# adaLN vectors as row sums over transposed weights, in a two-layer retention and attention trunk

## The chip, the cores and the metric

One core of a Trainium2 chip runs the whole kernel. The metric is the time of one execution on the device in microseconds; the median over runs is compared.

## The reference

A sequence of 512 tokens with 1024 features passes two layers. Layer 0 mixes tokens by multi-scale retention (4 heads), layer 1 by chunked attention with a relative bias (16 heads). Both start with an RMS norm that is modulated by a condition vector c, the same for all tokens, and both end with a gated residual:

```
cond = silu(c)                                   # [1024]
for i in range(2):
    mod = cond @ ada_w[i] + ada_b[i]             # [1024] x [1024, 3072]
    shift, scale, gate = split(mod, 3)
    h = rms_norm(x, norm_g[i]) * (1 + scale) + shift
    out = retention(h) if i == 0 else attention(h)   # h @ w_in, mixing, * silu gate, @ w_out
    x = x + gate * out
```

All data are float32. The six vectors (shift, scale and gate of both layers) are matrix-vector products with 24 MB of weights in all.

## The kernel before

TensorE does the large products in float32r. Every operand is split into two parts, a high one (a copy by ScalarE, `hi`) and a low one (a subtraction, mostly by VectorE, `lo`), and each 128x512 product is three matmuls. `load` fetches 512 rows by 512 columns of weights through SyncE's queue into one of two `raw` buffers (L258), and makes `whi` (L266, ScalarE) and `wlo` (L267); for output projections GpSimd first multiplies the weights by the gate (L263). In the last half of the last output projection GpSimd also does the low part (`low=nc.gpsimd`).

The products run as units of 12 matmuls. `go` runs a list of units; `at(u, fn)` hangs other work behind unit u. The tile framework then plans the order of every engine's queue with a timeline simulation, by the priority of program order and by when it takes data to be ready; `tc.issue_after` forces an order. A tile's `bufs` says how many buffers its tag has, and a tile whose buffer is still in use waits.

**The start.** h of layer 0 is made by quarters of the features. `norm_x` loads x, squares and scales it, and TensorE transposes it into `xT`. `prepare(s)` makes scale and shift of 256 features (`ada_256`), two rows of h of 128 features (L442) with their split, and the first weights for these rows. The eight 128x256 pieces of an adaLN weight are multiplied by cond, one value per partition, and added up: on VectorE (L412, L415) for all shifts and the first scale, on ScalarE and GpSimd (L418, L420) for the other scales. `column_sums` then sums over the partitions with matmuls against ones (L162). The products of quarter s (`first[0]`, the first values, and `first[1]`, the first queries) run while quarter s + 1 is prepared.

**The side vectors.** The gate of layer 0 and all vectors of layer 1 are made in 16 pieces, one behind every fourth unit of layer 0 (`side_piece`). Their weights go through `ada_load` (L126), 1 MB at a time, into the same two `raw` buffers as the projection weights; eight steps on VectorE (L148, L150) sum 512 columns. Layer 1's scale and shift are then transposed (L169) and reduced. A gate is split and spread to all partitions by two matmuls with ones (L201, L202); its bias is loaded by GpSimd (L141) into the first row of the sum.

```
for half in range(2):
    raw = ada_load(pool, layer, col, half)
    for k in range(4):
        ...
            nc.vector.scalar_tensor_tensor(acc, raw[:, k, :], c1, acc, ALU.mult, ALU.add)
```

Other lines that are named below: rotary products on VectorE (`rt`, L532, L537), head outputs of layer 0 (L618, L625), and in layer 1 the scores (`as`, L787), their addition of the bias with a running maximum (L790, one instruction that writes out and accumulates) and the transposed probabilities (`pth`, `ptl`).

Of the kernel before, what the change touches and what calls it, by code (L numbers as in the profile page):

```python
# [37 lines left out]
def f32(ap):  # L38
    return ap.bitcast(F32)
# [3 lines left out]
def hybrid_trunk_kernel(  # L43
# [3 lines left out]
    c_t: bass.AP,  # L47
    positions: bass.AP,
    norm_t: bass.AP,
    ada_w: bass.AP,  # L50
    ada_b: bass.AP,
# [24 lines left out]
    ct = cp.tile([P, NK], F32, name="ct")  # L76
    nc.sync.dma_start(ct, c_t)
# [21 lines left out]
    cond = cp.tile([P, NK], F32, name="cond")  # L99
    with tc.high_priority():  # L100
        nc.scalar.activation(cond, ct, AF.Silu)
# [8 lines left out]

    gs = cp.tile([P, 2, NK], F32, name="gs")
# [12 lines left out]
    def ada_load(pool, layer, col, half):  # L124
        raw = pool.tile([P, 4, 512], F32, tag="raw", name=f"ada_{layer}_{col}_{half}")
        nc.sync.dma_start(  # L126
            raw,
            ada_w[layer, half * 512 : (half + 1) * 512, col : col + 512].rearrange(
                "(k p) n -> p k n", p=P
            ),  # L130
        )
        return raw

    def ada_acc(pool, layer, col):
        """sum over k-tiles of cond * ada_w on every partition: [P, 512], in two steps;
        a gate's bias stands in the sum of the first partition."""
        acc = np_.tile([P, 512], F32, tag="acc", name=f"acc_{layer}_{col}", bufs=1)
        gate = col >= 2 * D
        if gate:
            nc.gpsimd.memset(acc, 0.0)  # L140
            nc.gpsimd.dma_start(acc[0:1, :], ada_b[layer : layer + 1, col : col + 512])  # L141
        for half in range(2):
            raw = ada_load(pool, layer, col, half)
            for k in range(4):
                kt = half * 4 + k
                c1 = cond[:, kt : kt + 1]
                if kt == 0 and not gate:
                    nc.vector.tensor_scalar(acc, raw[:, k, :], c1, None, ALU.mult)  # L148
                else:
                    nc.vector.scalar_tensor_tensor(acc, raw[:, k, :], c1, acc, ALU.mult, ALU.add)  # L150
            if half == 0:
                yield
        yield acc

    def column_sums(blocks, name, direct=False):
        """blocks: lists of [P, P]; the sums over their partitions, as [P, blocks]."""
        n, z = len(blocks), len(blocks[0])
        if direct:
            ps = pa.tile([P, n], F32, tag="pa", name=name)
            for j, parts in enumerate(blocks):  # L160
                for i, a in enumerate(parts):
                    mm = nc.tensor.matmul(  # L162
                        ps[:, j : j + 1], a, ones[:, 0:1], start=i == 0, stop=i == z - 1
                    )
            return ps, mm
        ps = pa.tile([P, n, z * P], F32, tag="pa", name=name)
        for j, parts in enumerate(blocks):
            for i, a in enumerate(parts):
                mm = nc.tensor.transpose(ps[:, j, i * P : (i + 1) * P], a, ident)  # L169
        sums = sp.tile([P, n], F32, tag=f"sums{n}", name=f"sums_{name}")  # L170
        nc.vector.tensor_reduce(sums, ps, mybir.AxisListType.X, ALU.add)
        return sums, mm

    def ada_finish(layer, col, accs, n):
        """n * 128 columns of scale or shift, summed over the partitions and laid over them."""
        c0 = col // P
        ps, mm = column_sums([[a[:, j * P : (j + 1) * P] for a in accs] for j in range(n)], f"mod_{layer}_{col}", layer == 0)
        if col < D:
            nc.vector.tensor_tensor(sh[:, layer, c0 : c0 + n], ps, bt[:, layer, c0 : c0 + n], ALU.add)
        else:  # L180
            tmp = sp.tile([P, n], F32, tag="mods", name="mods")
            nc.vector.tensor_tensor(tmp, ps, bt[:, layer, c0 : c0 + n], ALU.add)
            d0 = c0 - NK
            nc.vector.scalar_tensor_tensor(
                gs[:, layer, d0 : d0 + n], tmp, 1.0, ng[:, layer, d0 : d0 + n], ALU.add, ALU.mult
            )
        return mm

    def ada(pool, layer, col):
        """512 columns: scale and shift laid over the partitions, the gate on each of them."""  # L190
        for acc in ada_acc(pool, layer, col):
            if acc is None:
                yield
        if col < 2 * D:
            ada_finish(layer, col, [acc], 4)
        else:
            ps = pa.tile([P, 512], F32, tag="pa", name=f"gp_{layer}_{col}")
            hi = np_.tile([P, 512], F32R, tag="nat", name=f"gh_{layer}_{col}")
            lo = np_.tile([P, 512], F32R, tag="nat", name=f"gl_{layer}_{col}")
            split(hi, lo, acc)  # L200
            nc.tensor.matmul(ps, ones_r, hi, start=True, stop=False)  # L201
            nc.tensor.matmul(ps, ones_r, lo, start=False, stop=True)  # L202
            nc.scalar.activation(gates[layer][:, col - 2 * D : col - 2 * D + 512], ps, AF.Copy)
        yield

# [1 line left out]
    def norm_rows(t, tag, scalar=False):  # L207
        """x / rms(x), in two halves of the columns."""
# [39 lines left out]
    def load(parts, name, width=512, scale=None, w=None, k0=0, k1=4, low=None):  # L248
        """k-tiles k0..k1 of a piece of 4; parts: (columns of the tile, rows of the weights)."""
# [40 lines left out]
    class Chunk:  # L290
        """Columns of an input projection; cols: list of (columns of the tile, first column)."""
# [39 lines left out]
    # Products run as units of 12 matmuls; the other work is hung behind given units.  # L331
# [22 lines left out]
    def out_proj(name, w_out, row0, ys, gate, store=None, t_outer=False, done=None, rstd=None):  # L354
        ws = [None, None]

        def unit(half, t):
            csl = slice(half * 512, (half + 1) * 512)
            if ws[half] is None:
                ws[half] = load(  # L360
                    [(ALLC, w_out[row0 : row0 + 512, csl])], f"{name}_{half}", scale=gate[:, csl],
                    low=nc.gpsimd if store is not None and half else None,
                )
# [29 lines left out]
    with tc.tile_pool(name="st", bufs=1) as st:  # L393
        xT = st.tile([P, NK, S], F32, name="xT")

        def ada_256(col, name, vector, behind=None):
            raw = st.tile([P, NK, 256], F32, tag=f"ada_{name}", name=f"ada_0_{col}", bufs=3)
            for half in range(2):
                nc.sync.dma_start(
                    raw[:, half * 4 : half * 4 + 4, :],  # L400
                    ada_w[0, half * 512 : half * 512 + 512, col : col + 256].rearrange(
                        "(k p) n -> p k n", p=P
                    ),
                )
            accs = []
            for kt in range(NK):
                c1 = cond[:, kt : kt + 1]
                src = raw[:, kt, :]
                if vector and kt < 2:
                    acc = st.tile([P, 256], F32, tag=f"acc{kt}_{name}", name=f"acc{kt}_{col}")  # L410
                    accs.append(acc)
                    nc.vector.tensor_scalar(acc, src, c1, None, ALU.mult)  # L412
                elif vector:
                    acc = accs[kt % 2]
                    nc.vector.scalar_tensor_tensor(acc, src, c1, acc, ALU.mult, ALU.add)  # L415
                else:
                    with tc.issue_after(behind.ins) if behind else nullcontext():
                        nc.scalar.activation(src, src, AF.Copy, scale=c1)  # L418
                    if kt:
                        nc.gpsimd.tensor_tensor(raw[:, 0, :], raw[:, 0, :], src, ALU.add)  # L420
            return ada_finish(0, col, accs if vector else [raw[:, 0, :]], 2)
# [545 lines left out]
```

## Time and profile before

| what | value |
|---|---|
| median of 3 runs | 1000.54 us (996.72 to 1001.76) |
| span of the profiled execution | 996.1 us |
| mean granted TensorE clock | 0.986 |
| TensorE busy | 963.9 us (97%) |
| VectorE, ScalarE, GpSimd busy | 608.7, 384.3, 212.1 us |
| moved by DMA | 111.26 MB |

The span is from the first to the last instruction of one execution; of what lies around it the profile gives no time of its own, and the median of the runs is 4.4 us above it. Busy shares are averages over a start, two layers and a tail with different limits, so stretches and waits are read beside them.

### The profile page before, as it was taken

The page shows a single profiled execution, that of the slowest core. Times are in us where ns is not written, and L with a number is a line of the kernel's source. Part 1 is how long each engine was busy: PE and PEld are TensorE (multiplying, and loading weights), DVE is VectorE, ACT ScalarE, POOL GpSimd, SP SyncE. Part 2 cuts the span into 40 slices and gives each one's busy share as a digit, 9 for nine tenths or more (in the row PEclk, how much of TensorE's full clock was granted, in tenths as well). Part 3 has the DMA queues.
Part 4 walks back from the last instruction along what each step waited for, and adds up shares of the span by engine and source line. Part 5 has one row for each costly group of instructions (what it writes and reads, how often), then busy time and mean ns, then how long its engine had stood idle before and what let it go on. Part 6 is the DMA issues. An engine that isn't in the chain of part 4 may idle for free.

```text
span 996.1 us, 11965 instructions
## 1 busy us (share of the span) xinstructions
PE 963.9 (97%) x4572; PEld 803.9 (81%) x4572; DVE 608.7 (61%) x1012; ACT 384.3 (39%) x813; POOL 212.1 (21%) x205
## 2 busy tenths in 40 slices
PE   4999979999999999999999999999999999999988
PEld 3778868888778888888788888888888888888876
DVE  6977789558862563766445566545556346556683
ACT  6433413232223333426344445234543244444431
POOL 4810231004200103612100270002520012004520
PEclk8799989999999999999999999999999999999999
DMA  9645534653262222222232222223223232213202
GB/s 336 215 129 188 180 126 129 193 196 124 89 209 98 85 85 84 85 85 85 93 104 71 74 96 96 96 85 93 73 78 97 84 96 90 90 56 99 91 1 85
DMA packets 80537, 111.26 MB, mean 112 GB/s; under 512 B 12016, under 2 KB 44832, under 8 KB 80480
## 3 DMA queue, kind: packets, MB, share of 16 engines
q1 hardware_dynamic: 68368, 102.77, 31.3%
q0 software_dynamic: 10960, 5.63, 2.1%
q10 hardware_dynamic: 1152, 2.10, 0.6%
q8 instruction: 36, 0.59, 0.2%
q14 instruction: 21, 0.17, 0.1%
HBM read 108.32 MB, written 2.10 MB: 111 GB/s over the span
## 4 chain that ended last, share of the span: by engine, by line
PE 81%; DVE 8%; DMA 5%; issue 3%; POOL 1%; ACT 1%; SPq 0%; POOLq 0%; DVEq 0%; ACTq 0%
PE pm_aqk L277 6%; PE pm_aqk L275 6%; PE pm_aqk L276 6%; PE ao L827 3%; PE as L787 3%; PE pm_av L276 3%; PE pm_av L277 3%; PE pm_av L275 3%; PE po_a L277 3%; PE po_a L276 3%; PE po_a L275 3%; PE pm_ag L283 3%; DVE acc L150 3%; PE pm_ag L284 3%; PE pm_ag L285 3%; DMA ada<-in_ada_w_dram 3%
## 5 line engine op out<-in xcount | busy, mean ns | idle before, releaser
L275 PE MATMUL pm_aqk<-whi_aqk,hTh 128*128 128x512 f32 x256 | 101.8, 398 | 0.0
L277 PE MATMUL pm_aqk<-whi_aqk,hTl 128*128 128x512 f32 x256 | 100.5, 393 | 0.0
L276 PE MATMUL pm_aqk<-wlo_aqk,hTh 128*128 128x512 f32 x256 | 100.3, 392 | 0.0
L150 DVE SCALAR_TENSOR_TENSOR acc<-ada,cond,acc 128x512 f32<-128x512 f32 x60 | 52.9, 882 | 22.5 <-DMA ada<-in_ada_w_dram 11.5
L275 PE MATMUL pm_rv<-whi_rv,hTh 128*128 128x512 f32 x128 | 52.3, 413 | 5.4 <-ACT hTh L350 5.4
L277 PEld LDWEIGHTS pm_aqk<-whi_aqk,hTl 128*128 128x128 f32 x256 | 48.1, 188 | 10.1
L775 POOL DMA_DIRECT2D br<-in_att_bias_dram x16 | 13.4, 837 | 200.3 <-DVE nm L794 172.1
L275 PEld LDWEIGHTS pm_aqk<-whi_aqk,hTh 128*128 128x128 f32 x256 | 48.1, 188 | 9.5
L276 PEld LDWEIGHTS pm_aqk<-wlo_aqk,hTh 128*128 128x128 f32 x256 | 48.2, 188 | 9.3
L267 DVE TENSOR_TENSOR wlo_aqk<-raw_aqk,whi_aqk 128x2048 fp32r<-128x2048 f32 x16 | 36.6, 2289 | 30.3 <-ACT whi_aqk L266 30.3
L796 ACT ACTIVATE p<-p,nm 128x128 f32<-128x128 f32 (+1 forms) x64 | 35.9, 563 | 49.3 <-DVE nm L794 48.3
L263 POOL TENSOR_TENSOR raw_r<-raw_r,gate 128x2048 f32<-128x2048 f32 x8 | 39.5, 4937 | 72.1 <-DMA raw_r<-in_ret_w_out_dram 70.5
L275 PE MATMUL po_r<-whi_r,yh 128*128 128x512 f32 x128 | 51.8, 407 | 1.5 <-DVE rt L532 1.5
L790 DVE CUSTOM_DVE_ANT_0 p<-as,br 128x128 f32<-128x128 f32 (+1 forms) x64 | 30.4, 486 | 36.8 <-PE as L787 33.9
L276 PE MATMUL pm_rv<-wlo_rv,hTh 128*128 128x512 f32 x128 | 52.4, 409 | 0.0
L276 PE MATMUL po_r<-wlo_r,yh 128*128 128x512 f32 x128 | 51.7, 404 | 0.0
L277 PE MATMUL po_r<-whi_r,yl 128*128 128x512 f32 x128 | 51.6, 403 | 0.0
L285 PE MATMUL pm_rqk<-hTh,wlo_rqk 128*128 128x512 f32 x128 | 49.7, 391 | 1.8 <-DVE wlo_rqk L267 1.8
L283 PE MATMUL pm_ag<-hTh,whi_ag 128*128 128x512 f32 x128 | 50.7, 398 | 0.0
L283 PE MATMUL pm_rqk<-hTh,whi_rqk 128*128 128x512 f32 x128 | 50.7, 397 | 0.0
L284 PE MATMUL pm_ag<-hTl,whi_ag 128*128 128x512 f32 x128 | 50.4, 394 | 0.0
L277 PE MATMUL pm_rv<-whi_rv,hTl 128*128 128x512 f32 x128 | 50.3, 401 | 0.0
(219 smaller groups left out, 2622.3 us busy)
## 6 DMA issues: line engine op xcount, KB each, us to landing
ada<-in_ada_w_dram SPq DMA_DIRECT2D x16, 1024.0 KB, 5.1
raw_aqk<-in_att_w_in_dram SPq DMA_DIRECT2D x32, 512.0 KB, 4.6
ada<-in_ada_w_dram SPq DMA_DIRECT2D x16, 512.0 KB, 8.4
raw_rg<-in_ret_w_in_dram SPq DMA_DIRECT2D x8, 1024.0 KB, 5.1
raw_r<-in_ret_w_out_dram SPq DMA_DIRECT2D x8, 1024.0 KB, 5.0
raw_ag<-in_att_w_in_dram SPq DMA_DIRECT2D x8, 1024.0 KB, 5.4
raw_av<-in_att_w_in_dram SPq DMA_DIRECT2D x8, 1024.0 KB, 5.3
raw_a<-in_att_w_out_dram SPq DMA_DIRECT2D x8, 1024.0 KB, 5.1
```

Of the source, the lines that this page charges most:

```text
L150: nc.vector.scalar_tensor_tensor(acc, raw[:, k, :], c1, acc, ALU.mult, ALU.add)
L263: nc.gpsimd.tensor_tensor(raw, raw, scale.unsqueeze(1).broadcast_to([P, k1 - k0, width]), ALU.mult)
L267: (low or nc.vector).tensor_tensor(lo, raw, f32(hi), ALU.subtract)
L275: nc.tensor.matmul(ps, a_h, wh[:, k, :], start=first and k == 0, stop=False)
L276: nc.tensor.matmul(ps, a_h, wl[:, k, :], start=False, stop=False)
L277: nc.tensor.matmul(ps, a_l, wh[:, k, :], start=False, stop=last and k == 3)
L283: nc.tensor.matmul(ps, wh[:, k, csl], h, start=first and k == 0, stop=False)
L284: nc.tensor.matmul(ps, wh[:, k, csl], l, start=False, stop=False)
L285: nc.tensor.matmul(ps, wl[:, k, csl], h, start=False, stop=last and k == 3)
L787: nc.tensor.matmul(ps[:, :w0], a[:, qsl], b[:, :w0], start=z == 0, stop=z == 2)
L790: nc.vector.tensor_tensor_reduce(p[:, :w], ps[:, :w], br[:, S - w :], 1.0, -3.0e38, ALU.add, ALU.max, mx)
L796: nc.scalar.activation(p[:, :w], p[:, :w], AF.Exp, bias=nm, accum_out=sm)
```

## The change

The weights of the adaLN vectors come transposed from the host (`ada_t`, one row per feature), and cond lies on all partitions as a row of 1024. A vector's values of 128 features are then one VectorE instruction that multiplies a [128, 1024] tile of weight rows by cond and sums along the row into a column of `mod` (`ada_dot`). No sum over partitions is left for scale and shift. A gate has to be spread to all partitions: 128 values become a diagonal matrix (`diag`, two buffers), and TensorE multiplies it with ones in fp32, four times per 512 features. In the start VectorE does all of the sums and all steps that make h, weights come in 1 MB loads into six buffers, and the forced orders go. The side vectors have two buffers of their own (`ada`, 4 KB per partition); each block's load is hung four units ahead of its sum. The low part of the last weights goes to VectorE. Two one-column tiles share one tile of 64 columns, and the scratch for GpSimd's transfer descriptors shrinks from its default to 4096 bytes per partition.

```diff
-    ct = cp.tile([P, NK], F32, name="ct")
-    nc.sync.dma_start(ct, c_t)
+    cond = cp.tile([P, D], F32, name="cond")
+    nc.sync.dma_start(cond, c_row.broadcast_to([P, D]))
...
-        nc.scalar.activation(cond, ct, AF.Silu)
+        nc.scalar.activation(cond, cond, AF.Silu)
...
+    def ada_dot(raw, layer, block):
+        nc.vector.tensor_tensor_reduce(
+            raw, raw, cond, 1.0, 0.0, ALU.mult, ALU.add, mod[:, layer, block : block + 1]
+        )
+    def ada_finish(layer, b0, n):
+        m, b = mod[:, layer, b0 : b0 + n], bt[:, layer, b0 : b0 + n]
+        if b0 < NK:
+            nc.vector.tensor_tensor(sh[:, layer, b0 : b0 + n], m, b, ALU.add)
+            return
+        nc.vector.tensor_tensor(m, m, b, ALU.add)
+        if b0 < 2 * NK:
+            g0 = b0 - NK
+            nc.vector.scalar_tensor_tensor(
+                gs[:, layer, g0 : g0 + n], m, 1.0, ng[:, layer, g0 : g0 + n], ALU.add, ALU.mult
+            )
+            return
+        ps = pa.tile([P, n, P], F32, tag="pa", name=f"gp_{layer}_{b0}")
+        for j in range(n):
+            diag = np_.tile([P, P], F32, tag="diag", name=f"diag_{layer}_{b0 + j}", bufs=2)
+            nc.vector.tensor_scalar(diag, ident, m[:, j : j + 1], None, ALU.mult)
+            nc.tensor.matmul(ps[:, j, :], ones, diag, start=True, stop=True)
+        g0 = (b0 - 2 * NK) * P
+        nc.scalar.activation(
+            gates[layer][:, g0 : g0 + n * P], ps.rearrange("p a b -> p (a b)"), AF.Copy
+        )
...
-        (low or nc.vector).tensor_tensor(lo, raw, f32(hi), ALU.subtract)
+        nc.vector.tensor_tensor(lo, raw, f32(hi), ALU.subtract)
...
+        def ada_256(b0):
+            raw = st.tile([P, 2, D], F32, tag="ada", name=f"ada_0_{b0}", bufs=6)
+            nc.sync.dma_start(
+                raw, ada_t[0, b0 * P : (b0 + 2) * P, :].rearrange("(b p) k -> p b k", p=P)
+            )
+            for j in range(2):
+                ada_dot(raw[:, j, :], 0, b0 + j)
+            ada_finish(0, b0, 2)
...
-                (nc.vector if kt in (1, 3) else nc.gpsimd).tensor_scalar(
+                nc.vector.tensor_scalar(
...
-        _, h0 = prepare(0)
+        prepare(0)
         for s in range(3):
             ws = [ch.w for ch in first]
-            for u in range(4):
-                first[0].unit(s // 2, u, ks(s))
-            mm, _ = prepare(s + 1, None if s else h0)
-            with tc.issue_after(mm.ins):
-                new, first[1].w = first[1].w, ws[1]
-                for u in range(2):
-                    first[1].unit(s // 2, u, ks(s))
-                first[1].w = new
+            prepare(s + 1)
+            for ch, w in zip(first, ws):
+                new, ch.w = ch.w, w
+                for u in range(ch.n):
+                    ch.unit(s // 2, u, ks(s))
+                ch.w = new
...
+            tiny = rp.tile([P, 64], F32, name="tiny")
+            ifr, hpi = tiny[:, 0:1], tiny[:, 1:2]
...
-        for z in range(16):
-            at(now[0] + 2 + 4 * z, side_piece)
+        def side_load(layer, block):
+            raw = np_.tile([P, D], F32, tag="ada", name=f"ada_{layer}_{block}", bufs=2)
+            nc.sync.dma_start(raw, ada_t[layer, block * P : (block + 1) * P, :])
+            held[layer, block] = raw
+        def side_dot(layer, block):
+            ada_dot(held.pop((layer, block)), layer, block)
+            if block % 4 == 3:
+                ada_finish(layer, block - 3, 4)
+        held = {}
+        blocks = [(0, 16 + b) for b in range(8)]
+        blocks += [(1, b) for b in (*range(8, 16), *range(8), *range(16, 24))]
+        for z, (layer, block) in enumerate(blocks):
+            u = 2 + 2 * z if z < 8 else 20 + (z - 8) * 7 // 2
+            at(max(u - 4, 0), side_load, layer, block)
+            at(u, side_dot, layer, block)
...
-    nc = _bacc.Bacc("TRN2", target_bir_lowering=False, num_devices=1)
+    nc = _bacc.Bacc(
+        "TRN2", target_bir_lowering=False, num_devices=1, dynamic_dma_scratch_size=4096
+    )
```

## Rows read from the trace of the kernel before

**Rows 1.** Busy time by stretch: engine, busy us, instructions; granted clock, DMA share.
```profile
0.00:25.00 25.00, 10.46 (x55) 9.31 (x56) 15.15 (x40) 17.31 (x39) 10.93 (x26) 0.90 0.96 336
25.00:50.00 25.00, 22.69 (x86) 18.41 (x85) 23.54 (x36) 11.95 (x26) 20.16 (x22) 0.76 0.59 213
...
125.00:150.00 25.00, 19.85 (x78) 15.81 (x77) 21.39 (x26) 4.25 (x5) 8.19 (x3) 0.86 0.34 126
```

**Rows 2.** What TensorE waited for: us in total, times, longest us.
```profile
PE hp L431 <- DVE xn L225: 9.9, 1, 9.9
PE pm_rv L275 <- ACT hTh L350: 5.4, 2, 3.1
PE mod L169 <- DVE acc L150: 3.9, 1, 3.9
PE as L787 <- DVE ptl L351: 2.5, 1, 2.5
PE pm_rqk L285 <- DVE wlo_rqk L267: 1.8, 1, 1.8
...
PE po_r L275 <- DVE rt L532: 1.5, 2, 1.3
```

**Rows 3.** 9 to 57 us: VectorE alone, then all engines' instructions on adaLN tiles.
```profile
9.00:57.00 48.00, 43.34 (x81) 0.82 0.73 255
...
9.00:57.00 48.00, 1.85 (x12) 2.29 (x12) 23.36 (x40) 9.87 (x24) 18.61 (x21) 0.82 0.73 255
```

**Rows 4.** VectorE in order of time: start, us, line, operation, idle time before.
```profile
14.52 3.24 DVE L415 SCALAR_TENSOR_TENSOR acc<-ada,cond,acc 128x256 f32<-128x256 f32 x8
...
18.34 1.22 DVE L267 TENSOR_TENSOR wlo_rv<-raw_rv,whi_rv 128x1024 fp32r<-128x1024 f32 x1
...
21.86 0.69 DVE L351 TENSOR_TENSOR hTl<-h,hTh 128x512 fp32r<-128x512 f32 x1 [1.18 <-ACT hTh L350]
...
24.08 5.41 DVE L415 SCALAR_TENSOR_TENSOR acc<-ada,cond,acc 128x256 f32<-128x256 f32 x6
```

**Rows 5.** All engines and DMA from 11 to 37 us.
```profile
11.00:37.00 26.00, 19.02 (x95) 15.93 (x94) 24.64 (x48) 18.91 (x41) 15.04 (x18) 0.87 1.08 388
```

**Rows 6.** The chain of waits, 40 to 56 us: start, us, what.
```profile
40.65 1.44 PE mod L162 x6
...
45.28 0.43 PE pm_rv L275
...
48.09 0.23 PE pm_rv L275
```

**Rows 7.** VectorE in layer 1: an instruction that accumulates, 512 columns.
```profile
967.60 0.68 DVE L790 CUSTOM_DVE_ANT_0 p<-as,br 128x512 f32<-128x512 f32 x1
968.21 0.08 DVE L790 DVE_READ_ACCUMULATOR2_ANT mx<- 128x1 f32 x1
```

**Rows 8.** TensorE in order of time: idle time before and who ended it.
```profile
21.88 0.79 PE L275 MATMUL pm_rv<-whi_rv,hTh 128*128 128x512 f32 x1 [3.10 <-ACT hTh L350]
...
60.47 0.39 PE L275 MATMUL pm_rv<-whi_rv,hTh 128*128 128x512 f32 x1
...
142.22 0.52 PE L169 MATMUL mod<-ident,acc 128*128 128x128 f32 x3 [3.88 <-DVE acc L150]
```

**Rows 9.** Idle time of engines before adaLN steps, and a wait of SyncE's queue.
```profile
  DMA ada<-in_ada_w_dram: 17.8, 8
...
SPq L258 <- DVE wlo_aqk L267: 189.2, 15, 22.3
```

**Rows 10.** GpSimd and VectorE at the same time, at 124 and at 961 us.
```profile
123.59 5.11 POOL L263 TENSOR_TENSOR raw_r<-raw_r,gate 128x2048 f32<-128x2048 f32 x1 [0.56 <-DVE yl L625]
...
124.16 5.08 DVE L150 SCALAR_TENSOR_TENSOR acc<-ada,cond,acc 128x512 f32<-128x512 f32 x1
...
960.45 4.58 POOL L267 TENSOR_TENSOR wlo_a<-raw_a,whi_a 128x2048 fp32r<-128x2048 f32 x1 [13.40 <-ACT whi_a L266]
...
961.09 4.09 DVE L799 TENSOR_SCALAR p<-p,ri 128x256 f32<-128x256 f32 x1
```

More of the change, by code (lines that the diff above doesn't have):

```diff
@@ L1 @@
 import math
-from contextlib import ExitStack, nullcontext
+from contextlib import ExitStack
 import numpy as np
@@ L46, in hybrid_trunk_kernel @@
     x: bass.AP,
-    c_t: bass.AP,
+    c_row: bass.AP,
     positions: bass.AP,
     norm_t: bass.AP,
-    ada_w: bass.AP,
-    ada_b: bass.AP,
+    ada_t: bass.AP,
     ada_bt: bass.AP,
@@ L97, in hybrid_trunk_kernel @@
     nc.gpsimd.memset(mhalf, -0.5)
-    cond = cp.tile([P, NK], F32, name="cond")
     with tc.high_priority():
-        nc.scalar.activation(cond, ct, AF.Silu)
+        nc.scalar.activation(cond, cond, AF.Silu)
     kq = cp.tile([P, 1], F32, name="kq")
@@ L109, in new_h @@
         hT["l"] = hp.tile([P, NK, S], F32R, tag="hTl", name=f"hTl_{layer}")
+    mod = cp.tile([P, 2, 24], F32, name="mod")
     gs = cp.tile([P, 2, NK], F32, name="gs")
@@ L121, in rstd_of @@
         return rs
[L124 to L130, printed above, removed]
-        )
[L132 to L169, printed above, removed]
+    def ada_dot(raw, layer, block):
+        nc.vector.tensor_tensor_reduce(
+            raw, raw, cond, 1.0, 0.0, ALU.mult, ALU.add, mod[:, layer, block : block + 1]
+        )
@@ L170, in column_sums @@
+    def column_sums(blocks, name):
+        n = len(blocks)
+        ps = pa.tile([P, n, P], F32, tag="pa", name=name)
+        for j, a in enumerate(blocks):
+            nc.tensor.transpose(ps[:, j, :], a, ident)
         sums = sp.tile([P, n], F32, tag=f"sums{n}", name=f"sums_{name}")
         nc.vector.tensor_reduce(sums, ps, mybir.AxisListType.X, ALU.add)
[L172 to L204, printed above, removed]
+        return sums
@@ L245, in norm_tile, with load @@
             nc.vector.tensor_tensor(hT["l"][:, ksl, tsl], h, f32(hT["h"][:, ksl, tsl]), ALU.subtract)
-    def load(parts, name, width=512, scale=None, w=None, k0=0, k1=4, low=None):
+    def load(parts, name, width=512, scale=None, w=None, k0=0, k1=4):
         if w is None:
@@ L361, in unit @@
                     [(ALLC, w_out[row0 : row0 + 512, csl])], f"{name}_{half}", scale=gate[:, csl],
-                    low=nc.gpsimd if store is not None and half else None,
                 )
@@ L394, in hybrid_trunk_kernel @@
         xT = st.tile([P, NK, S], F32, name="xT")
[L396 to L421, printed above, removed]
+        def ada_256(b0):
[6 more added lines that the diff above has]
+            ada_finish(0, b0, 2)
         def norm_x():
@@ L434, in norm_x, with prepare @@
                     )
-        def prepare(s, behind=None):
-            ada_256(D + s * 256, "scale", s == 0, behind)
-            mm = ada_256(s * 256, "shift", True)
+        def prepare(s):
+            ada_256(NK + 2 * s)
+            ada_256(2 * s)
             for kt in (2 * s, 2 * s + 1):
                 h = np_.tile([P, S], F32, tag="nat", name=f"h_0_{kt}")
-                (nc.vector if kt in (1, 3) else nc.gpsimd).tensor_scalar(
+                nc.vector.tensor_scalar(
                     h, xT[:, kt, :], gs[:, 0, kt : kt + 1], sh[:, 0, kt : kt + 1], ALU.mult, ALU.add
                 )
-                last = split(hT["h"][:, kt, :], hT["l"][:, kt, :], h)
+                split(hT["h"][:, kt, :], hT["l"][:, kt, :], h)
             for ch in first:
                 ch.load(s // 2, ks(s))
-            return mm, last
         def ks(s):
@@ L489, in rope_tables @@
             nc.gpsimd.dma_start(posi, positions.broadcast_to([P, S]))
-            ifr = rp.tile([P, 1], F32, name="ifr")
+            tiny = rp.tile([P, 64], F32, name="tiny")
+            ifr, hpi = tiny[:, 0:1], tiny[:, 1:2]
             nc.gpsimd.dma_start(ifr, inv_freq)
-            hpi = rp.tile([P, 1], F32, name="hpi")
             nc.gpsimd.memset(hpi, math.pi / 2)
@@ L630, in norm_y @@
         def norm_y(n):
-            ps, _ = column_sums([[rstd[n][:, t * P : (t + 1) * P]] for t in range(NT)], f"ss_{n}")
+            ps = column_sums([rstd[n][:, t * P : (t + 1) * P] for t in range(NT)], f"ss_{n}")
             ms = sp.tile([P, NT], F32, tag="ms4", name=f"ms_{n}")
@@ L650, in outp @@
             return out_proj(f"r{n}", ret_w_out, n * 512, lambda: yy[n], gates[0], rstd=lambda: rstd[n], **kw)
-        side = [ada(wp, *a) for a in (
-            (0, 2 * D), (0, 2 * D + 512), (1, D), (1, D + 512), (1, 0), (1, 512),
-            (1, 2 * D), (1, 2 * D + 512),
-        )]
-        def side_piece():
-            if side:
-                g = side[0]
-                k = side_n[0] = side_n[0] + 1
-                next(g)
-                if k % 2 == 0:
-                    side.pop(0)
-        side_n = [0]
-        for z in range(16):
-            at(now[0] + 2 + 4 * z, side_piece)
+        def side_load(layer, block):
[13 more added lines that the diff above has]
+            at(u, side_dot, layer, block)
         rope_tables()
@@ L892 @@
 _INS = [
-    "x", "c_t", "positions", "norm_t", "ada_w", "ada_b", "ada_bt", "ret_w_in", "ret_gn_t", "ret_w_out",
+    "x", "c_row", "positions", "norm_t", "ada_t", "ada_bt", "ret_w_in", "ret_gn_t", "ret_w_out",
     "att_w_in", "att_qg_t", "att_kg_t", "att_bias", "att_w_out", "inv_freq", "decay",
@@ L936 @@
         "x": np.asarray(x)[0],
-        "c_t": np.asarray(c).reshape(NK, P).T,
+        "c_row": np.asarray(c).reshape(1, D),
         "positions": np.asarray(positions),
         "norm_t": np.asarray(norm_g).reshape(2, NK, P).transpose(2, 0, 1),
-        "ada_w": ada_w,
-        "ada_b": ab,
+        "ada_t": np.asarray(ada_w).transpose(0, 2, 1),
         "ada_bt": ab.reshape(2, 24, P).transpose(2, 0, 1),
```

## Prediction

> **What bounds the kernel now.** I read the busy time by stretch first. TensorE is busy nearly all the time except in two places: the first 50 us, where 0:25 has 10.46 us of work and 25:50 a mean granted clock of 0.76, and 125:150, with 19.85 us of 25 and a clock of 0.86 [rows 1]. Any gain must come from there, or from a stall too short to show in a stretch.
>
> The waits of TensorE, longest in total first, name them [rows 2]: 9.9 us for normalised x before the first transposes, 5.4 us for the rounded half of h, 3.9 us for an adaLN accumulation (L150), 2.5 us for a split in the last layer, 1.8 us for a weight split, 1.5 us for the rotary products. All of these producers sit on VectorE or right behind it.
>
> In the start, 9 to 57, VectorE is busy 43.34 of 48 us; 23.36 us of that works on adaLN tiles, beside 9.87 us of ScalarE and 18.61 us of GpSimd on the same tiles [rows 3]. The reader is to see that the two engines disturb each other: eight L415 steps take 3.24 us, 0.405 each, while GpSimd is quiet, and six take 5.41 us, 0.90 each, while it adds [rows 4]. DMA moves 388 GB/s from 11 to 37 us [rows 5]: the 13 MB that the start needs (x 2, adaLN 8, weights 3) take 33.5 us at that rate, and beginning at 2 to 5 us they bring the last block at 36 to 39. Until then data limits the start, VectorE and TensorE after it.
>
> A TensorE pause is paid twice. In the chain of waits a 512-column matmul takes 0.43 us at 45 us and 0.23 at 48 [rows 6]: the granted clock is at its lower level, 1.2 GHz, after the stalls ahead of it, and at 2.4 later.
>
> **The change, part by part.** *Row sums.* 512 columns of one vector cost eight VectorE steps before, plus column sums on TensorE. Now four instructions of 128x1024 do it, with the sum in `mod`. No such instruction is in the trace. From below: a plain two-input step of 128x1024 takes 1.22 us [rows 4]. From the same family: L790, which also writes out and accumulates, takes 0.68 at 512 columns and 0.08 for reading the accumulator [rows 7], so one more 512 columns (1.22 - 0.69 = 0.53) give 0.68 + 0.53 + 0.08 = 1.29. From above: twice the plain step, 2.44. I take 1.3, by the row of the same operation.
>
> A rule speaks for the upper end. The Trainium skill (Vector Engine (DVE) Microarchitecture Reference, section Points that are easy to get wrong) says that a scalar-tensor-tensor step with two SBUF sources that aren't bf16 runs at half rate, for want of a port for the accumulator. The quiet L415 steps have two such sources and 0.405 us for 256 columns, not half the rate of the plain step; but they don't use the accumulator, and L790 reads one source from PSUM, so no run here shows the case itself. By the rule the 16 blocks of the start would take 39 us instead of 21.
>
> *Start.* Layer 0's scale and shift are 16 blocks: 16 x 1.3 = 20.8 us of VectorE in place of 23.36, and the 9.87 us on ScalarE, the 18.61 on GpSimd and 26 column-sum matmuls (two instructions each, 0.24 at the lower clock [rows 6]) go. All eight h steps move to VectorE, six of them from GpSimd: at 0.45 us (one source, so less than the 0.69 of a two-input step of that width [rows 4]) that is +2.7 us. GpSimd being quiet, nothing else on VectorE is stretched. From about 11 us VectorE then has 20.8 (sums) + 8 x 0.45 (h) + 8 x 0.6 (low halves, the 0.69 overlaps the next by 0.09 [rows 4]) + 4 x 1.15 and 4 x 0.6 (weight splits) + 4 (small steps and x) = 40.2 us, and ends at 51 rather than 57.
>
> For TensorE I follow its order. First product: now 21.88 [rows 8], after an h step on GpSimd; with VectorE's shorter one and sums instead of column sums, about 20. Each of the four feature quarters has 36 matmuls, 8.2 us at 0.227. Quarter 0 starts at 20, about 12 of them at 0.43 (now the same), ends at 31. Quarter 1 has its h at about 28: 31 to 39. Quarter 2 has h at 38 and its weights at 39, since its buffers come free when quarter 1's value products end: 39 to 47.5. Quarter 3 needs h from the last two loads, which land at about 39 by the DMA rate, then four sums: 47 to 48, so it ends at 56.5. In the trace it starts at 60.47 and lasts as long [rows 8], ending at 68.7. Gain 12; as VectorE has no slack left there I take 10.5. Bounds: 2 (only the first product earlier) and 13.
>
> *The condition vector on all partitions.* A 512 KB load ahead of x instead of 4 KB, and a 128x1024 SiLU. At 388 GB/s [rows 5] it delays x and all behind it by 1.3 us; the SiLU takes 1 us of ScalarE ahead of the squares of x. Against that GpSimd no longer issues bias loads between the steps of the norm. Together 0 to 2 us; it is inside the 10.5. A source row read 128 times might come slower; the first scale block lands at 11, so 6 us are covered.
>
> *Own buffers.* The side vectors shared the two `raw` buffers and SyncE's queue with the weights, one MB at a time, issued when a buffer came free. VectorE stood still for them eight times, 17.8 us [rows 9]; once this reached TensorE, up to 142.22: 3.88 us [rows 8], 1.3 more for the rotary products behind it on VectorE [rows 2], then about 12 matmuls at the lower clock, 12 x 0.2 = 2.4 (the mean clock of 0.86 [rows 1] says 25 x 0.14 x 2 = 7 us at that level, pauses included). With loads of 512 KB issued four units ahead (4 x 12 x 0.227 = 10.9 us) and 1.3 us of work per block, none is late. Gain 7.5 (bounds 0 and 8). What is late next is the 4.6 to 5 us in which a GpSimd gate product holds a VectorE step: L263 123.59 to 128.7, L150 124.16 to 129.2 [rows 10]. This stays.
>
> *Gates by diagonals.* 16 VectorE steps of 128x128 (about 0.25 us) and 16 fp32 matmuls replace eight 128x512 matmuls (1.8 us) and four pairs of split steps. An fp32 product is two instructions; each costs at least the 0.12 of a column sum at full clock (half of 0.24) and at most a 512-column matmul, 0.23: 3.8 to 7.3 us. Net I add 2.5 us to TensorE (bounds 1 and 6: two `diag` buffers tie VectorE to TensorE's place, and a late VectorE holds TensorE). In layer 1, 16 transposes go; I leave them uncounted.
>
> *The last split on VectorE.* At 960.45 GpSimd runs it for 4.58 us and holds a 256-column VectorE step for 4.09 [rows 10]; TensorE waits 2.5 us [rows 2] and, as after the other pauses, restarts at the lower clock, for which I put 1 us. On VectorE it takes twice the 1.22 of half its width [rows 4], less overlap 2.3 us, and holds no one longer. Gain 2.5 (bounds 0 and 3.5).
>
> *The rest.* Shared tile for two tiny columns, smaller descriptor scratch, no forced issue order: nothing by any row; the work stays and few transfers come from GpSimd.
>
> **Sum.** -10.5 - 7.5 - 2.5 + 2.5 = -18. I add 1.5 for the 1.8 us wait for a weight split [rows 2], which moves to a place where VectorE has more to do. The instruction order is planned anew, so +-4. Span 996.1 - 16.5 = 979.6. The three runs shown are 996.7, 1000.5 and 1001.8; their median is 4.4 above the span. Keeping that distance: **984**.
>
> **Rivals.**
> 1. *VectorE stays the bound in the start*: sums at 2.44 us, or rotary tables and value splits that can't follow. At 2.44, 16 blocks add 18 us: VectorE ends near 69, quarter 3 ends at 75, 6.5 late instead of 12 early. With the 7.5, 2.5 and -2.5 of the rest the time is about 1000; with a mere half of the start's gain lost, 989. The half rate is what the skill's rule above would bring. For it: VectorE 43.34 of 48 busy [rows 3]. Against it: L790's row [rows 7].
> 2. *Every stall goes*: 13 + 8 + 3.5 - 1 = 23.5, and no new wait: 977. Also 973 if the short waits elsewhere shrink.
> 3. *Slower: sums at the head of VectorE's queue wait for late loads.* 32 block loads lie in SyncE's queue among weight loads that wait up to 22.3 us for their buffers [rows 9], twice the lead of 10.9 us; a sum in front of VectorE then holds splits and rotations. One such stall costs TensorE 3.9 + 1.3 + 2.4 = 7.6 us, as at 138. Against a gain of 18 it decides from the third on; with four it is 1000.5 - 16.5 + 30 = 1014. Against it: sums wait for one 512 KB load, not for 1 MB behind two weight tiles.
> 4. *No change*: the planner hides the start's gain in waits at about 70 us, and the gates take the rest: 1000.
>
> **How the numbers follow.** Main case 0.56: 978 to 990, predicted 984. Rival 2: 0.16, rival 1 with half the gain lost 0.12, with the sums at half rate 0.05, rival 4 0.05, rival 3 0.06. Within 0.5% (995.5 to 1005.5) is about what a measurement tells from no change. Faster 0.84, same 0.10, slower 0.06. The range holds the main case, rival 2 and the milder rival 1: 971 to 995; outside it lie 0.16.
>
> **What would show it.** Right: one 128x1024 sum near 1.3 us; no GpSimd adds before 57; first product near 20, the fourth quarter ended near 57; no TensorE wait above 2 us from 110 to 150 and a clock of 1.00 there; no GpSimd split near the end. Wrong: sums above 2 us; VectorE idle for `ada` loads; TensorE waiting for `diag`, `vl` or rotary products; the low clock in more stretches than before.

## The result: slower by 1%, where a gain of 1.6% was forecast

The changed kernel takes 1008.08 us (median of 4 runs, 1007.40 to 1010.44) against 998.85 us for the kernel before, run beside it (996.72 to 1001.76). The ratio is 1.0101, with a 95% interval of 1.0073 to 1.0130. The prediction was 984 us, range 971 to 995, with a chance of 0.06 for slower. It was wrong in sign. The profiled execution took 1008.13 us; its span rose from 996.1 to 1006.4 us, though TensorE's busy time fell from 963.9 to 961.0 us and VectorE's from 608.7 to 595.7: TensorE stands idle 13.2 us longer, and its mean granted clock falls from 0.986 to 0.980.

Busy time by stretch, changed kernel (columns as in [rows 1]):

```profile
0.00:25.00 25.00, 8.49 (x36) 6.93 (x37) 12.53 (x29) 16.04 (x33) 8.84 (x20) 0.86 0.93 350
25.00:50.00 25.00, 21.41 (x82) 17.06 (x81) 24.96 (x51) 6.40 (x10) 0.64 (x1) 0.86 0.81 311
50.00:75.00 25.00, 18.52 (x72) 14.42 (x71) 20.66 (x41) 5.44 (x8) 1.69 (x5) 0.82 0.64 194
75.00:100.00 25.00, 24.49 (x105) 19.78 (x105) 23.96 (x38) 8.16 (x9) 0.00 (x0) 0.98 0.84 303
100.00:125.00 25.00, 23.83 (x120) 20.12 (x118) 22.91 (x34) 7.26 (x10) 5.10 (x1) 1.00 0.63 216
125.00:150.00 25.00, 18.44 (x82) 15.58 (x83) 19.23 (x29) 6.95 (x10) 6.45 (x5) 0.86 0.61 184
150.00:175.00 25.00, 20.90 (x85) 16.75 (x85) 22.90 (x30) 6.73 (x7) 6.44 (x2) 0.86 0.28 95
```

The loss lies before 175 us. 50:75, 125:150 and 150:175 now have 18 to 21 us of TensorE work and a granted clock of 0.82 to 0.86, and VectorE is busy for 20.7 to 25.0 us of every 25 from 25 to 125. What TensorE waited for (as [rows 2]), the waits above 2 us:

```profile
PE hp L368 <- DVE xn L181: 10.0, 2, 9.5
PE ss L157 <- POOL sq L550: 6.3, 1, 6.3
PE pm_rqk L239 <- DVE vl L307: 4.2, 1, 4.2
PE po_r L231 <- DVE x L327: 4.1, 1, 4.1
PE pm_rv L231 <- ACT hTh L306: 4.0, 1, 4.0
PE pm_rv L231 <- ACT whi_rv L222: 3.6, 1, 3.6
PE hp L368 <- ACT xn L179: 2.5, 2, 2.0
PE pm_rqk L241 <- DVE wlo_rqk L223: 2.3, 1, 2.3
```

The wait for an adaLN accumulation (3.9 us) and that for the last split (2.5 us) are gone, as intended. Waits of 6.3, 4.2, 4.1 and 3.6 us stand in their place, none of them for an adaLN vector. The chain of waits says what lies behind them; these are its pieces on side vectors and one beside them (start, us, what):

```profile
53.54 5.83 DMA ada<-in_ada_t_dram
59.39 1.23 DVE ada L124
60.65 4.93 DMA ada<-in_ada_t_dram
73.62 5.63 DMA ada<-in_ada_t_dram
...
101.42 4.16 DMA ada<-in_ada_t_dram
...
110.60 7.59 DMA ada<-in_ada_t_dram
118.21 5.29 DVE ada L124
...
128.10 6.77 DMA ada<-in_ada_t_dram
137.31 2.13 DVE ada L124
139.61 1.66 DVE yl L559
```

From 53 to 140 us the end is set in good part by loads and sums of side vectors (over the whole chain, the start's included, such loads make 3.8% and such sums 4.4% of the span, 38 and 44 us). With two buffers a load starts when a sum has freed one, and lands 3 to 8 us later in these pieces; the next sum waits for it with the rest of VectorE's queue behind. What SyncE's queue waits for at a side load is mostly a row sum (us in total, times, longest):

```profile
SPq L589 <- DVE mod L124: 63.6, 23, 6.8
```

All 32 side sums are over by 162 us; before, the L150 steps ran from 61.1 to 282.5 us. VectorE in order of time, behind the start and at 118 us:

```profile
59.39 1.23 DVE L124 CUSTOM_DVE_ANT_0 ada<-ada,cond 128x1024 f32<-128x1024 f32 x1 [2.29 <-DMA ada<-in_ada_t_dram]
60.54 0.08 DVE L124 DVE_READ_ACCUMULATOR2_ANT mod<- 128x1 f32 x1
...
61.62 1.23 DVE L124 CUSTOM_DVE_ANT_0 ada<-ada,cond 128x1024 f32<-128x1024 f32 x1 [0.27 <-DMA ada<-in_ada_t_dram]
...
65.60 1.22 DVE L124 CUSTOM_DVE_ANT_0 ada<-ada,cond 128x1024 f32<-128x1024 f32 x1 [1.68 <-DMA ada<-in_ada_t_dram]
...
67.36 1.28 DVE L307 TENSOR_TENSOR vl<-pm_rv,vh 128x512 fp32r<-128x512 f32 x2
...
118.21 5.29 DVE L124 CUSTOM_DVE_ANT_0 ada<-ada,cond 128x1024 f32<-128x1024 f32 x1 [0.27 <-DMA ada<-in_ada_t_dram]
...
124.58 0.28 DVE L525 TENSOR_TENSOR pf<-st,dec 128x128 f32<-128x128 f32 x1
```

Between 57 and 67 us three sums stand ahead of the value split `vl`, with 4.2 us of idle time for their loads. TensorE, in order of time, waits those 4.2 us (third line), after waits at 23.54 and 46.00 in the start:

```profile
23.54 0.80 PE L231 MATMUL pm_rv<-whi_rv,hTh 128*128 128x512 f32 x1 [4.01 <-ACT hTh L306]
...
46.00 2.08 PE L231 MATMUL pm_rv<-whi_rv,hTh 128*128 128x512 f32 x4 [3.59 <-ACT whi_rv L222]
...
68.19 0.77 PE L239 MATMUL pm_rqk<-hTh,whi_rqk 128*128 128x512 f32 x1 [4.21 <-DVE vl L307]
```

### The profile page after: what moved, and what is told of

The parts are those of the page before. It is cut to its first block, busy times and chain, and to the rows that moved or that the text cites. A ratio compares the mean times of both kernels' runs of the same rounds, so it can differ in the third digit from the quotient of the medians.

```text
span 1006.4 us, 11781 instructions
## 1 busy us (share of the span) xinstructions
PE 961.0 (95%) x4528; PEld 800.4 (80%) x4528; DVE 595.7 (59%) x1023; ACT 373.1 (37%) x785; POOL 183.5 (18%) x169
## 3 DMA queue, kind: packets, MB, share of 16 engines
q0 software_dynamic: 10832, 5.62, 2.0%
## 4 chain that ended last, share of the span: by engine, by line
PE 82%; DVE 10%; DMA 5%; issue 1%; ACT 1%; POOL 1%; SPq 0%; DVEq 0%; POOLq 0%
PE pm_aqk L231 6%; PE pm_aqk L233 6%; PE pm_aqk L232 6%; DVE ada L124 4%; DMA ada<-in_ada_t_dram 4%; PE as L723 3%; PE ao L763 3%; PE po_a L231 3%; PE po_a L233 3%; PE po_a L232 3%; PE pm_av L231 3%; PE pm_av L232 3%; PE pm_av L233 3%; PE po_r L231 3%; PE po_r L232 3%; PE po_r L233 3%
## 5 line engine op out<-in xcount | busy, mean ns | idle before, releaser
L124 DVE CUSTOM_DVE_ANT_0 ada<-ada,cond 128x1024 f32<-128x1024 f32 x48 | 62.7, 1328 | 12.6 <-DMA ada<-in_ada_t_dram 12.6
L223 DVE TENSOR_TENSOR wlo_aqk<-raw_aqk,whi_aqk 128x2048 fp32r<-128x2048 f32 x16 | 41.0, 2562 | 30.4 <-ACT whi_aqk L222 30.4
L240 PE MATMUL pm_rqk<-hTl,whi_rqk 128*128 128x512 f32 x128 | 52.2, 408 | 0.0
```

The source lines that it names most:

```text
L124: nc.vector.tensor_tensor_reduce(raw, raw, cond, 1.0, 0.0, ALU.mult, ALU.add, mod[:, layer, block : block + 1])
L223: nc.vector.tensor_tensor(lo, raw, f32(hi), ALU.subtract)
L240: nc.tensor.matmul(ps, wh[:, k, csl], l, start=False, stop=False)
```

## Experiments

**Theory A:** the shared weight buffers had held the side sums back. With buffers of their own they come up early in VectorE's order, crowd it from 38 to 163 us, and stand before splits and rotations that TensorE needs at once. **B:** side loads that come late, whatever the order. **C:** the new start is at fault. **D:** side loads take the queue from weight loads.

**paced.** Each side load goes behind the newest weight load on SyncE's queue, and each side sum behind the newest weight split on VectorE (`newest` is set where these are issued):

```diff
-            nc.sync.dma_start(raw, ada_t[layer, block * P : (block + 1) * P, :])
+            with tc.issue_after(newest["load"].ins):
+                nc.sync.dma_start(raw, ada_t[layer, block * P : (block + 1) * P, :])
...
-            ada_dot(held.pop((layer, block)), layer, block)
+            with tc.issue_after(newest["split"].ins):
+                ada_dot(held.pop((layer, block)), layer, block)
```

> The changed kernel, with each side sum and its load queued behind the newest weight split (VectorE) and the newest weight load (SyncE) that the program had issued when its unit came up; nothing else is changed. Theory A (the own buffers take away the pacing, the 32 side sums run from 38 to 162 us instead of up to 340 us and crowd VectorE, whose splits and rotations then hold TensorE): the waits for vl, wlo_rqk, sq and x between 63 and 163 us go or halve, and the time falls by 12 to 20 us from 1008, to 988 to 996. Theory B (late loads at the head of VectorE's queue are the cause, 12.6 us of idle time): loads stay behind weight loads, so 1003 to 1012. Theory C (the start is at fault): 1005 to 1010.

Measured: 982.99 us (982.34 to 985.93), 0.9866 of before [0.9844, 0.9888], 5 us below the lowest that I expected under Theory A. The order of 32 sums and loads is worth 25 us of 1008 (23 by the ratios to before). The row sums by line (duration min/median/max, then first and last start; the first 16 are the start's), and two stretches:

```profile
L124 DVE CUSTOM_DVE_ANT_0 ada<-ada,cond x48: 1211/1218/2319, 13.7 to 365.9; 128x1024 f32<-128x1024 f32 x48
```

```profile
50.00:75.00 25.00, 23.37 (x104) 19.03 (x103) 20.33 (x35) 8.32 (x10) 0.56 (x2) 1.00 0.60 200
...
125.00:150.00 25.00, 25.00 (x114) 20.64 (x113) 22.91 (x28) 6.83 (x7) 4.62 (x1) 1.00 0.35 126
```

The last sum now starts at 366 us (160.4 in the changed kernel), TensorE is busy throughout from 100 to 400 us, and the clock is 1.00 there. Of the waits above, those for `sq`, `vl`, `x` and `whi_rv` are gone and that for `wlo_rqk` is 1.6 us.

**shared_buffers.** The own buffers alone undone: pairs of blocks through the weights' buffers, at the old units.

```diff
-            raw = np_.tile([P, D], F32, tag="ada", name=f"ada_{layer}_{block}", bufs=2)
+            raw = wp.tile([P, 2, D], F32, tag="raw", name=f"ada_{layer}_{block}")
...
+            at(now[0] + 2 + 4 * z, side_pair, layer, block)
```

> The changed kernel with the own buffers alone undone: the 32 side blocks come as 16 transfers of 1 MB in pairs, through the two buffers of the weights, hung behind the units at which the kernel before hung its 16 pieces (2, 6, 10, ..., 62). Row sums, diagonal gates, the new start and the new tail stay; there is no pacing. Theory A (own buffers took away what had held the sums back): the sums spread over about 60 to 285 us again, and the time comes close to that of old_side or below, 984 to 996, with a wait left where a weight split is late behind a side pair. If it is the row sums themselves, or the diagonals, that crowd VectorE: the time stays over 1003.

Measured: 990.61 us (987.21 to 991.97), 0.9920 [0.9892, 0.9948]. Its sums last to 256 us:

```profile
L124 DVE CUSTOM_DVE_ANT_0 ada<-ada,cond x48: 1208/1220/3398, 13.7 to 256.0; 128x1024 f32<-128x1024 f32 x48
```

So about 18 us come back without the own buffers and with the pairs and units that go with them; the run does not part these three. By the ratios 5 us are left to paced; TensorE waits here 3.4 us for a weight split and 2.1 for a diagonal, and the clock is 0.86 in 50:75.

**pace_sums** and **pace_loads.** One half of the pacing each.

> The changed kernel with only half of the pacing: each of the 32 side sums is put behind the newest split of a weight piece on VectorE, as in the run named paced, and their loads stay where they were (issued as soon as one of the two buffers is free). Theory A (early sums crowd VectorE between 38 and 163 us; the loads themselves do no harm): the sums again run from about 65 to 366 us, no wait for the order of the gate column sum or of the value splits near 64 us, time within 0.5% of paced, 979 to 988. Rival D (the side loads get ahead of weight loads in the queue and delay those, so the loads have to be paced): the time stays above 990, with TensorE waiting for whi or wlo of a weight piece.

> The changed kernel with the other half of the pacing: each side load is put behind the newest weight load on the queue of transfers, and the sums stay free. A sum can't run before its load, so under Theory A most of the crowding goes too, but the order on VectorE is still the planner's and a sum may stand at the head of the queue and wait for its paced load: 983 to 995, with VectorE idle for side loads some 5 to 15 us in all. Under rival D (the loads are what has to be paced) it equals paced, 983. Under Theory B of before (late loads at the head of VectorE's queue are what costs) it is slower than the changed kernel, over 1010.

Measured: sums alone 983.65 us (982.30 to 984.49), 0.9854 [0.9840, 0.9869], as good as both; loads alone 991.52 us (989.11 to 992.02), 0.9930 [0.9913, 0.9946]. D falls: the loads need no pacing. B falls as it stood: pace_loads lets VectorE idle for side loads longer than any other run (us in total, times, longest),

```profile
DVE ada L124 <- DMA ada<-in_ada_t_dram: 57.7, 21, 7.7
```

against 12.6 us in the changed kernel, and is 17 us faster. An idle VectorE costs only where TensorE is about to need what is queued behind: in pace_loads that shows above all at one place, TensorE's wait for the value split near 64 us, 4.3 of 5.1 us. My 5 to 15 us of idle time was far too low. Whether more than two side buffers, with the sums left free, would help was not run.

**half_sums.** The changed kernel with each side sum over the first half of its row.

```diff
-            ada_dot(held.pop((layer, block)), layer, block)
+            ada_dot(held.pop((layer, block))[:, :512], layer, block)
```

> The changed kernel with each of the 32 side sums over the first 512 of its 1024 columns alone (it leaves out half of the row in each, so the modulation of those vectors is that of half a row); loads, buffers and the calls are the same. A sum then takes about 0.70 us, not 1.22, so VectorE has 32 x 0.53 = 17 us less to do between 38 and 163 us. Theory A, in its form that VectorE's load in that stretch is the harm: a good part of the 25 us that pacing gives comes back, 990 to 1000. If the place of the sums in the order is the harm whatever their length (a split or a rotation waits behind a sum that waits for its load): within 0.5% of the changed kernel, 1003 to 1010.

Measured: 1001.25 us (997.32 to 1003.47), 1.0030 [1.0014, 1.0045]. With 17 us less to do on VectorE, 7 of the 25 us come back, less than I put for the load and more than for the place alone. TensorE's waits are mostly of the same kinds, some shorter, and that for a weight split longer:

```profile
PE pm_rqk L241 <- DVE wlo_rqk L223: 4.1, 1, 4.1
...
PE ss L157 <- POOL sq L550: 3.9, 1, 3.9
...
PE po_r L231 <- DVE rt L466: 1.9, 1, 1.9
PE pm_rqk L239 <- DVE vl L307: 1.9, 2, 1.5
```

VectorE's idle time for side loads rose from 12.6 to 23.0 us, so a part of the freed time went into waiting for loads that were as long as before, and the order was planned anew. The run shows that length is a part of the loss; that place is the larger part (sums that wait for a load, with other work behind them) rests on pace_sums, and the exact shares stay open.

**new_side_alone.** The kernel before with the new side vectors only; start and tail old.

> The kernel before with only the side vectors made in the new way (row sums, own buffers, gates by diagonals; the condition vector is loaded to all partitions besides, behind the small loads of GpSimd, and the descriptor scratch is small); start and tail as before. Theories A and B: the early sums cost here too, 1005 to 1016 against 998.9 for before. Theory C: 990 to 997, since the stall at 138 us goes.

Measured: 1019.91 us (1018.75 to 1020.68), 1.0227 [1.0211, 1.0242]. That is above the 1005 to 1016 that I expected: this part by itself costs more than the whole change. The side sums end at 169 us here too. C falls.

**side_paced_alone.** The same with the pacing of paced.

> The kernel before with the new side vectors alone (row sums, own buffers, diagonal gates), as in the run named new_side_alone (1.0227 of before), and with the pacing of the run named paced: each side sum behind the newest weight split, each side load behind the newest weight load. The start and the tail are the old ones. Theory A: the 22 us that the new side cost by itself go, and the prediction's terms for the side hold: own buffers -7.5, gates by diagonals +2.5, so ratio 0.995, 991 to 997, with no wait for an adaLN vector at 138 us and the clock at 1.00 in 125:150. If pacing only works with the new start (which frees VectorE before 60 us): the time stays above that of before, over 1002.

Measured: 993.48 us (992.05 to 1001.84), 0.9967 [0.9946, 0.9988]: 26 us come back, and pacing needs no new start. The stretch in which the kernel before had 19.85 us and a clock of 0.86 [rows 1]:

```profile
125.00:150.00 25.00, 23.90 (x115) 19.72 (x114) 20.36 (x27) 6.44 (x10) 10.79 (x6) 1.00 0.21 71
```

**old_side.** The changed kernel with the old side vectors; start and tail new.

> The changed kernel with the old way of making the side vectors (1 MB pieces through the shared raw buffers, eight steps for 512 columns, sums over partitions on TensorE), the start and the tail as changed. Theories A and B: the start keeps its 5 us at the end of quarter 3 and the tail its 2 to 3, the old stall at about 138 us may come back: 986 to 996. Theory C: no better than 1003.

Measured: 994.55 us (993.02 to 996.15), 0.9964 [0.9951, 0.9977], no more than the tail gives (next run). The first product of the retention's gate (`pm_rg`) is 3.1 us earlier than before (78.5 against 81.6), the first of its output projection (`po_r`) is not (144.1 against 144.0): TensorE waits again at 140 to 144, behind an accumulation and then rotations, and the start's gain is lost there.

```profile
140.07 0.41 PE L164 MATMUL mod<-ident,acc 128*128 128x128 f32 x2 [1.23 <-DVE acc L196]
144.07 0.77 PE L301 MATMUL po_r<-whi_r,yh 128*128 128x512 f32 x1 [3.59 <-DVE rt L536]
```

**new_tail_alone.** The kernel before with the last split on VectorE.

> The kernel before with only the low part of the last weights moved from GpSimd to VectorE. All theories: the 2.5 us wait at 963 us and the slow clock behind it go, 995 to 997.5 against 998.9, a ratio of 0.996 to 0.9985; if the planner's new order matters more, within 3 us of before.

Measured: 994.69 us (993.40 to 999.55), 0.9972 [0.9956, 0.9989], 2.8 us by the ratio (1.1 to 4.4). The split takes 2.29 us, and the wait of 2.5 us [rows 2] is gone.

```profile
965.15 2.29 DVE L267 TENSOR_TENSOR wlo_a<-raw_a,whi_a 128x2048 fp32r<-128x2048 f32 x1 [0.35 <-ACT whi_a L266]
```

**cond_late, h_scalar, norm_first.** Three trials on the start, each on top of paced.

```diff
# cond_late: the load and SiLU of cond stand behind the loads of x
# h_scalar
-                nc.vector.tensor_scalar(
-                    h, xT[:, kt, :], gs[:, 0, kt : kt + 1], sh[:, 0, kt : kt + 1], ALU.mult, ALU.add
-                )
+                nc.scalar.activation(
+                    h, xT[:, kt, :], AF.Identity, bias=sh[:, 0, kt : kt + 1], scale=gs[:, 0, kt : kt + 1]
+                )
# norm_first: rs of the last tile of x
+                with tc.issue_after(last_rs[-1].ins):
                     ada_dot(raw[:, j, :], 0, b0 + j)
```

> Paced, with the load of the condition vector on all partitions (512 KB) put behind the four tiles of x on the queue of transfers, and its SiLU with it. The prediction put this part at 0 to 2 us. If the load ahead of x costs its 1.3 us: the squares of x start near 4.7 us rather than 6.47, the first product about 1.5 us earlier than 23.5, and the time is 1 to 2 us below paced, 981 to 982. If the first product is held by GpSimd's steps and by the order on VectorE behind it, or the start is bound by the last adaLN loads: no difference, 982 to 984. The planner writes the order of the start anew for it, which can cost or give 2 us by itself.

> Paced, with the eight steps of the start that form h moved from VectorE to ScalarE (which had 7.6 us of work in 25:50). If VectorE is still the bound of the start (24.96 of 25 us busy in 25:50): 8 x 0.45 = 3.6 us go from its chain, quarters 2 and 3 begin 2 to 3 us earlier, the time is 2 to 3 us below paced, 980 to 981. If TensorE's queue is bound there by the landing of loads or by the rotary tables and value splits after it: no change that can be told, 982 to 984. If ScalarE, with its weight roundings, becomes the later one: 984 to 987.

> Paced, with the first row sums put behind the GpSimd step that gives the last scale of x, so that no sum runs on VectorE while GpSimd works on the norm. In paced, those two GpSimd steps take 1.20 and 1.42 us beside the sums, 0.37 and 0.67 without. If that stretching is what makes the first product late: the two steps together fall to about 1 us, the first product comes 1 to 1.5 us earlier than 23.5, and the time is up to 1 us below paced. If the first product is bound by the weight split in front of h on VectorE: the first product stays at 23 to 24, and VectorE, starting its sums a microsecond later, makes the time 983 to 985.

Measured: cond_late 984.08 us (0.9859 [0.9843, 0.9876]), h_scalar 982.07 us (0.9846 [0.9831, 0.9860]), norm_first 984.00 us (0.9862 [0.9845, 0.9878]); none can be told from paced by its ratio. In cond_late the squares of x do start at 4.80 rather than 6.47 us, but the first product comes at 24.24, later than in paced (23.47): the planner ordered the start otherwise (GpSimd's last two norm steps begin at 15.70, not 13.74), and the gain was not kept. In h_scalar quarter 2 starts 1.25 us earlier (43.28 against 44.53) and then TensorE waits 2.46 us, not 1.63, for the next weight split near 64: VectorE gave way and the next stage took it back; its median is the lowest of all. norm_first did not do what it was to: the forced order did not hold between GpSimd and VectorE, the sum still began at 13.7 us, beside GpSimd's two steps, which stayed as long:

```profile
13.79 1.23 POOL L119 TENSOR_SCALAR ms<-s 128x1 f32<-128x1 f32 x1 [1.07 <-DVE s L176]
15.10 1.42 POOL L121 TENSOR_TENSOR rs<-ms,mhalf 128x1 f32<-128x1 f32 x1
```

Whether that stretching sets the first product stays open.

## Why the prediction was wrong, step by step

- **The step that failed: "Own buffers ... With loads of 512 KB issued four units ahead ... and 1.3 us of work per block, none is late. Gain 7.5."** I took the sums to run at the units they are hung behind (2 to 100, to 366 us as paced shows). The shared buffers had also been what held them there. Without them the sums ran by 162 us, their loads came late, through two buffers, and the cost was about 25 us (paced against changed). Undoing the buffers, with the pairs and units of before, gave about 18 back. Against old_side, which has the same start and tail, the new side vectors cost 1.0101 / 0.9964, 1.4% or 14 us, where these terms were to gain 5. The allowance "+-4" for an order planned anew was where this was hidden.
- **Rival 3** had the place right, sums at the head of VectorE's queue that wait for loads. Its reason (side loads stuck behind weight loads that wait for their buffers) is not what the chain shows: side loads wait for side buffers, because the sums stand too early. Pacing the sums alone cures it. My 0.06 rested on "one 512 KB load, not 1 MB", an argument about length where order decides.
- **The terms themselves, once order is kept.** Side (7.5 - 2.5 = 5 forecast): side_paced_alone gives 0.33%, 3.3 us. Tail (2.5): 2.8. Start (10.5): what is left of paced is 1 - 0.9866 / (0.9967 x 0.9972) = 0.73%, about 7 us, `pm_rg` beginning 6.2 us earlier (75.4 against 81.6). This is a remainder and not the start by itself: with the old side vectors the start gave next to nothing (old_side against new_tail_alone, 0.9964 / 0.9972). Together 13, where the forecast was 18, or 16.5 net of the "+1.5". So 984 is close to the time of paced, in part by luck: it was counted from a median before of 1000.5, and that beside paced was 997.9. It doesn't make the forecast right for this kernel.
- **Row sum at 1.3 us:** right. 1.22 us and 0.08 for the accumulator, 1.15 from start to start. Rival 1's half rate, 2.44, did not come. The Trainium skill (Vector Engine (DVE) Microarchitecture Reference, Points that are easy to get wrong) has that rate for a scalar-tensor-tensor step with two SBUF sources that aren't bf16. The profile lists the row sum as CUSTOM_DVE_ANT_0: the trace shows that a multiply with row sum of two fp32 SBUF sources is not slowed so, and no run tests the rule for the step that it names.
- **VectorE done with the start at 51:** right in paced (its last low half of h ends at 50.80 + 0.69 = 51.5). In the changed kernel it is 56.5, four side sums (4 x 1.15) having gone in between.
- **First product at 20, quarter 3 at 47 to 48:** mis-sized. 23.54 and 55.66 us. I put the condition vector's 512 KB "inside the 10.5" as 0 to 2; the squares of x began 1.8 us later (6.50 against 4.71), and GpSimd's last two norm steps took 1.19 and 1.42 us beside the sums, not 0.23 and 0.55. Quarter 2 then waited 3.59 us for rounded weights at 46.00, where I had its weights at 39.
- **Gates by diagonals, +2.5:** TensorE's busy time on them is 4.9 us in paced against 3.3 before, and no wait for `diag` is left there; the net 3.3 us of the side is the only measure of the term's rest.
- **What would show it:** the sentences on what would be wrong named VectorE idle for `ada` loads, TensorE waiting for `vl`, and the low clock in more stretches; all three came.

## What to carry to other kernels

A shared buffer can be a brake as well as a bottleneck: before giving background work buffers of its own, look at what else holds it to its place, and put an explicit order in the brake's stead. Here ordering each background step behind the newest urgent one on its engine turned 1008 us into 983. Where a planner writes the order, forecast the place of moved work first and its duration second: a row sum (1.22 us against 1.3) and the last split (2.29 against 2.3) took about what I had put for them, and the sign was wrong.

## What was not expected of the hardware

That a gate product of GpSimd holds a VectorE step was forecast ("this stays"). What was not is the way from there to TensorE, twice in the changed kernel. A row sum that takes 1.22 us by itself took 5.29 while GpSimd's gate product ran (118.21 above). Behind it on VectorE stood one more row sum and then the last masked scores (`pf`, 124.58 above), for which TensorE had been done at 117.5. Only then did GpSimd issue the load of its next decay mask (`dec`), and it stood still for 10.56 us until that had landed. GpSimd, in order of time:

```profile
117.31 5.10 POOL L219 TENSOR_TENSOR raw_r<-raw_r,gate 128x2048 f32<-128x2048 f32 x1 [52.50 <-DVE ptl L307]
125.15 0.84 POOL L506 DMA_DIRECT2D dec<-in_decay_dram  x1 [2.74 <-DVE pf L525]
136.55 0.14 POOL L507 MEMSET dec<- 64x64 f32 x1 [10.56 <-DMA dec<-in_decay_dram]
136.77 5.62 POOL L550 TENSOR_TENSOR sq<-sq,sq 128x512 f32<-128x512 f32 x3
```

The squares that it then adds had been ready by 132.9. TensorE waited 6.3 us for their sum, the longest new wait. The three additions took 5.62 us beside a row sum and steps of `y` on VectorE, against 4.10 in the kernel before: 1.5 us of the wait, and the rest is their late start.

The second gate product came together with two diagonals on VectorE, which took 4.83 us instead of 0.48:

```profile
154.57 5.03 POOL L219 TENSOR_TENSOR raw_r<-raw_r,gate 128x2048 f32<-128x2048 f32 x1 [0.29 <-ACT gate L148]
```

```profile
155.04 4.83 DVE L145 TENSOR_SCALAR diag<-ident,mod 128x128 f32<-128x128 f32 x2
```

Behind them on VectorE stood one more row sum, rotary products and the `x` for which TensorE waits 4.1 us. In paced a gate product holds a weight split as long, and TensorE does not wait from 100 to 135 us: there too it is the place that costs, not the holding.

```profile
104.47 5.60 DVE L225 TENSOR_TENSOR wlo_rqk<-raw_rqk,whi_rqk 128x2048 fp32r<-128x2048 f32 x1 [1.21 <-ACT whi_rqk L224]
```

At the start a single-column GpSimd step stretched from 0.23 us before to 1.19 us beside a row sum.
